# Modulation vectors and x loaded behind the second projection's weights, and queries in tiles of their own, in a two-layer trunk

## The chip, the cores and the metric

The kernel runs on one core of a Trainium2 chip as a single program. The metric is the time of one execution on the device in microseconds, the median of several runs. The kernel before takes 1648.96 us (three runs, 1647.87 to 1651.08).

The core has five engines, each with an instruction stream that is worked off in order: PE (TensorE, matrix products), DVE (VectorE), ACT (ScalarE), POOL (GpSimd) and SP (SyncE, which here only issues transfers). An instruction that waits holds up all that stand behind it on its engine. Work tiles lie in SBUF, products arrive in PSUM, and 16 DMA engines move data between SBUF and the chip's memory (HBM).

## The reference

Two layers over 512 latent tokens and 256 context tokens, width 1024. Layer 0 has a pooling and gated-recurrence mixer, layer 1 attention with grouped keys, normalised queries and keys and rotary positions. Behind each stands a SwiGLU network of hidden width 2816. Norms stand on both sides of each part, and their scale, shift and gate are a modulation worked out from c. Cut to what matters here:

```python
m = silu(c) @ ada_w[l] + ada_b[l]                 # 6 vectors of 1024; for the context from c_ctx
f = swiglu(rmsnorm(x) * (1 + sc2) + sh2, w_in, w_out)
x = x + g2 * rmsnorm(f)                           # end of layer 0
h = rmsnorm(x) * (1 + sc1) + sh1                  # start of layer 1
q, k, v = split(h @ att_w_in)                     # 8 heads of queries, 2 of keys and values, 128 wide
q, k = grid_rope(rmsnorm(q)), grid_rope(rmsnorm(k))
```

## The kernel before

All activations lie with features on partitions and tokens in columns: columns 0 to 256 are the context, 256 to 768 the latent tokens. Each matrix product is three products of rounded halves: with w = whi + wlo and x = hh + hl, `mm3` (L185 to L187) adds whi·hh, whi·hl and wlo·hh in PSUM. Weights are loaded by SyncE as they are into one of four buffers `raw` (`load`, L113) and split there: ScalarE rounds them to `whi` (L641), VectorE subtracts and writes `wlo` (L642), after which the buffer is free. The split halves (a slot) lie in two tiles `w`, every third slot in an extra tile `w3`.

The stretch at issue begins where the hidden columns of layer 0's network are done. 22 blocks of hidden columns were written by SyncE from `gs` to memory (`gd`, L751) and come back as `g`, `hh`, `hl`, loaded by GpSimd (L786, L806). The second projection (`ffn0`) takes them in four chunks of 7, 8, 3 and 4 blocks. In a chunk it goes over eight output blocks n, two to a slot of weights in chunks 0 and 1 (`fo`), and in each over 256 and 512 columns (`outs`). Chunk 0's sums are copied out of PSUM by ScalarE (`y`, L732), those of the later chunks are added by VectorE (`y`, L734). Four PSUM buffers serve this. The context is in chunk 3 the last of three groups of 256 columns.

Beside chunks 0 and 1 VectorE works out 24 of the 48 columns of layer 1's modulation: SyncE loads a block of rows (`adat`, 512 KB) into a `raw` buffer, and VectorE multiplies it with the activated vectors `cb` and sums (L366), twice for the first 16 columns, once for the last 8. The first of two products writes what nobody reads to a second `raw` buffer (`junk`). `load_cb` loads the vectors for both streams to all partitions (L373), and ScalarE activates them (L374). The columns are a generator that `tick` advances by a credit for each piece of matrix work; it sets the program's order, from which a scheduler makes each engine's order.

In chunk 3 each group of columns, when done, goes through the norm of the network's output with the addition to `x` (`x` comes back from memory by a load in `Byg.add`, L80; two buffers for three groups), and then the norm of layer 1's input, which makes `hh` and `hl` (L256, L257). For a norm ScalarE squares (`sq`), VectorE adds (`ss`, L233), PE sums over partitions (L204), GpSimd takes the root (`rr`, L210), PE spreads it (L219), and VectorE scales (`u`). The additions to `x` stand on GpSimd (L298). Then `att_proj` makes queries: for each head and group of 256 columns 24 products, a square `sq` and a scaled copy of PSUM (L910, L912) into a tile that takes over the name `y`. Later the sums of the squares are taken by PE, and the head is rotated: SyncE copies it by parts (`sw`, L880), VectorE multiplies and adds, ScalarE rounds it to `qh`. Four heads of the first latent group come ahead of the second group's.

Of the kernel before, what the change touches and what calls it, by code (L numbers as in the profile page):

```python
# [8 lines left out]
F32 = mybir.dt.float32  # L9
F32R = mybir.dt.float32r  # L10
# [41 lines left out]
class Cols:  # L52


    def __init__(self, c, l):
        self.c, self.l = c, l
# [2 lines left out]
        return self.c[k][:, a:b] if b <= CTX else self.l[k][:, a - CTX:b - CTX]  # L59


class Full:


# [7 lines left out]
class Byg:  # L72


    def __init__(self, pool, tag, bufs):
        self.pool, self.tag, self.bufs, self.t, self.pool_nc = pool, tag, bufs, {}, None

    def add(self, a, src):
        t = self.t[a // 256] = self.pool.tile([128, KD, 256], F32, tag=self.tag, name=self.tag, bufs=self.bufs)
        self.pool_nc.sync.dma_start(out=t, in_=src[:, :, a:a + 256])  # L80
        return t

    def __call__(self, k, a, b):
# [9 lines left out]
class Trunk:  # L93
# [648 lines left out]
    def ffn0(self, y, h, closed, done, top):  # L742

        nc = self.nc
        gd = [self.dp.tile([128, 2, NT], F32, name=f"gd{j}") for j in range(KH)]

        def put(j):
            def f(a, b, src):
                t = self.tmp.tile([128, 2, 384], F32R, tag="gs", name="gs", bufs=2)
                self.split(t[:, 0, :b - a], t[:, 1, :b - a], src)  # L750
                nc.sync.dma_start(out=gd[j][:, :, a:b], in_=t[:, :, :b - a].bitcast(F32))  # L751
            return f

        w3 = self.pool("w3")
        self.w3 = w3.__enter__()
        tmp = self.pool("ftmp")
        self.tmp = tmp.__enter__()
        w = {}
        for i, (a, b) in [(i, g) for i in range(3) for g in G3[:2]] + [(i, G3[2]) for i in range(3)]:
            if a == G3[2][0] and i == 0:  # L760
                self.finish()
                closed()
                tp = self.pool("tx", side="right")
                t = self.wino_x(y, tp.__enter__())
                self.load_cb(self.tmp.tile([128, 1024], F32, name="cb0"), 1024)
            self.finish_for(a, b)
            if i not in w:
                w[i] = self.wslot(self.a["w_fi"][0, i], 2048)
            self.hidden(w[i], h, a, b, put(i))

        def ada1(m0, m1, cost):
            for m in range(m0, m1):
                self.ada_cols(m)
                yield cost

        self.along("ada", ada1(24, 48, 9.0))
        for j in range(3, KH - 1):
            self.wino_hidden(self.wino_w(self.a["w_fi"][0, j]), h, t, put(j))
        self.finish()
        tp.__exit__(None, None, None)  # L780
        self.left = []
        self.np = top.enter_context(self.pool("nrm1", side="right"))
        with self.pool("g2", side="right") as gp:
            def gload(j, k):
                t = gp.tile([128, 2, NT], F32R, tag=f"g{k}", name=f"g{k}")
                nc.gpsimd.dma_start(out=t, in_=gd[j].bitcast(F32R))  # L786
                return t

            def two(ts):
                return [lambda k, a, b, p=p: ts[k][:, p, a:b] for p in range(2)]  # L790

            g = [two([gload(j, j) for j in range(7)])]
            wl = self.wslot(self.a["w_fi"][0, KH - 1], 2048)
            for a, b in SG:
                self.hidden(wl, h, a, b, put(KH - 1))
            tmp.__exit__(None, None, None)
            with self.pool("x2", side="right") as xp:
                x = Byg(xp, "x", 2)
                x.pool_nc = nc
                cb = xp.tile([128, 2048], F32, name="cb1")  # L800
                self.load_cb(cb, 2048)
                self.along("ada", ada1(0, 24, 5.5))
                gb = self.htiles()
                for k in range(KD):
                    for p in range(2):
                        nc.gpsimd.dma_start(out=gb[p](k, 0, NT), in_=gd[7 + k][:, p, :].bitcast(F32R))  # L806
                g.append(gb)
                for ci in range(3):
                    if ci == 2:
                        ts = [gload(15 + k, k) for k in range(7)]  # L810
                        g += [two(ts[:3]), two(ts[3:])]
                    for n in range(KD):
                        if n % PER[FCH[0][ci]] == 0:
                            wo = self.fo(0, ci, n)
                        for a, b in GS:
                            self.outs(0, ci, g[ci], y, n, wo, a, b)
                            self.tick((b - a) * FCH[0][ci] / 800)
                self.finish()
                wo = [self.fo(0, 3, n) for n in (0, 4)]
                h1 = self.htiles()  # L820
                for a, b in GL + GS[:1]:
                    for n in range(KD):
                        self.outs(0, 3, g[3], y, n, wo[n // 4], a, b)
                        self.tick(4 * 0.32)
                    self.along((a, 0), done(x, h1, a, b))
                self.finish()
        self.w3 = None
        w3.__exit__(None, None, None)
        return h1
# [52 lines left out]
        (nc.gpsimd if WE & 4 else nc.vector).tensor_tensor(out=sw, in0=sw, in1=self.sin[:, s], op=ALU.mult)  # L882
        nc.vector.tensor_tensor(out=t, in0=t, in1=sw, op=ALU.add)

    def att_proj(self, h, yp):

        nc, ap = self.nc, self.ap
        self.cos = ap.tile([128, LAT], F32, name="cos")
        self.sin = ap.tile([128, LAT], F32, name="sin")
        nc.sync.dma_start(out=self.cos, in_=self.a["cos"])  # L890
        nc.sync.dma_start(out=self.sin, in_=self.a["sin"])
        self.kh = [ap.tile([128, NT], F32R, name=f"kh{i}") for i in range(ATT_KV)]
        self.kl = [ap.tile([128, NT], F32R, name=f"kl{i}") for i in range(ATT_KV)]
        self.vh = ap.tile([128, NCH, 256], F32R, name="vh")
        self.vl = ap.tile([128, NCH, 256], F32R, name="vl")
        self.rs = ap.tile([128, 2, ATT_H, 4], F32, name="rs")
        self.q = Full(yp, KD, F32, "y")

        def queries(w, hd, a, b):
            pt = self.ps()  # L900
# [155 lines left out]
    def run(self):  # L1056
        tc, nc, a = self.tc, self.nc, self.a
        with self.pool("const") as cp, self.pool("small", 2) as self.sm, self.pool("raw", 4) as self.rawp, \
# [12 lines left out]
            self.kvp.__exit__(None, None, None)  # L1071
            with self.psum(mm=("mm", 4), aux=("aux", 4)):
                self.layer1(mx)
            self.yctx.__exit__(None, None, None)

    def psum(self, **m):
        @contextlib.contextmanager
# [11 lines left out]
    def layer0(self):  # L1089
# [36 lines left out]
        with contextlib.ExitStack() as top:  # L1126
            npool = self.pool("nrm1", side="right")
            self.np = npool.__enter__()
            xpool = self.pool("x", side="right")
            x = Byg(xpool.__enter__(), "x", 3)  # L1130
            x.pool_nc = nc
            y = Full(yp, KD, F32, "y")
            for s, _ in G3:
                x.add(s, a["x"])
# [19 lines left out]
                npool.__exit__(None, None, None)  # L1154

            self.h1 = self.ffn0(y, h, closed, done, top)
            self.kvp = self.pool("kv")
            self.ap = self.kvp.__enter__()
            self.att_proj(self.h1, yp)
            assert not self.ada_left  # L1160

    def layer1(self, mx):
        nc, a = self.nc, self.a
        self.sb = SB2
        with self.pool("nrm2", side="right") as self.np, self.pool("x1", side="right") as xp:
            x = cols(None, xp, KD, F32, "x")
            y = Full(self.yp, KD, F32, "y")
            for k in range(KD):
                nc.sync.dma_start(out=x.l[k], in_=self.xs[:, k, :])
            h = self.htiles()  # L1170
# [162 lines left out]
```

## Time and profile before

| | |
|---|---|
| median of three runs | 1648.96 us (1647.87 to 1651.08) |
| profiled execution | 1650.64 us, its span 1648.6 us |
| PE busy | 1545.3 us, 94% of the span, 10656 matmuls |
| VectorE, ScalarE, GpSimd busy | 1004.0 (61%), 647.0 (39%), 122.6 us (7%) |
| mean granted clock of PE | 0.974 of full speed |
| read and written in memory | 178.28 and 24.64 MB |

PE is near its full time, so the profile is read for the places where PE waits, and for what PE waits for: a line "PE mm L185 <- ACT whi" says that products of line 185 stood until ScalarE's `whi` was there. The granted clock is a share of full speed; 0.50 is 1.2 GHz, 1.00 is 2.4 GHz. Line numbers are those of the kernel before. The mean of a group of rows mixes its forms where it says so.

### The profile page before, as it was taken

Reading aid. Unit: us, or ns where it says so; the run is one execution under the profiler, and the core shown is the slowest. Engines: PE = TensorE matmul, PEld = TensorE weight load, DVE = VectorE, ACT = ScalarE, POOL = GpSimd, SP = SyncE. Lnnn points to the kernel's source line nnn. Section 1 sums busy time; section 2 is a strip of 40 time slices with the busy share of each in tenths; the row PEclk is TensorE's granted clock in tenths of the full one; section 3 lists DMA queues with packets and bytes.
Section 4 is the critical chain, followed back from the end, with each engine's and each line's share of the span. In section 5 each row is a group of like instructions: output and inputs, shape, how many; then the busy total and the mean of one; then the engine's idle time right before and its main releaser. Section 6 shows DMA issues by size and latency. Waiting matters only on the chain.

```text
span 1648.6 us, 26592 instructions
## 1 busy us (share of the span) xinstructions
PE 1545.3 (94%) x10656; PEld 1385.3 (84%) x10656; DVE 1004.0 (61%) x1923; ACT 647.0 (39%) x1228; POOL 122.6 (7%) x163
## 2 busy tenths in 40 slices
PE   5999998999999999999599994999999999999997
PEld 2877776789899999999488894989999888888886
DVE  5366575644789898873465467678947523343345
ACT  3334343254555444442121133457845332222222
POOL 0000000001200000002000013220004000000002
PEclk9999999999999999999799996999999899999998
DMA  9142242341515555438878213230022223322311
GB/s 364 51 154 78 78 129 78 122 154 64 153 66 200 183 191 187 160 129 277 282 252 285 77 40 103 82 111 27 2 103 78 86 93 103 102 92 88 101 52 51
DMA packets 78154, 207.25 MB, mean 126 GB/s; under 512 B 7760, under 2 KB 35920, under 8 KB 77904
## 3 DMA queue, kind: packets, MB, share of 16 engines
q1 hardware_dynamic: 73568, 188.07, 35.1%
q0 software_dynamic: 4320, 17.30, 3.0%
q8 instruction: 83, 1.36, 0.3%
q14 instruction: 39, 0.32, 0.1%
q10 hardware_dynamic: 144, 0.20, 0.0%
HBM read 178.28 MB, written 24.64 MB: 123 GB/s over the span
## 4 chain that ended last, share of the span: by engine, by line
PE 62%; DVE 6%; POOL 2%; ACT 2%; issue 1%; DMA 1%; SPq 0%; POOLq 0%; DVEq 0%; ACTq 0%
PE mm L185 20%; PE mm L186 19%; PE mm L187 19%; DVE ss L233 1%; DMA raw<-adat 1%; PE pp L1022 1%; POOL x L298 1%; PE aux L204 1%; PE aux L219 1%; PE st L185 1%; PE st L187 1%; PE st L186 1%; DVE u L294 0%; DVE wlo L642 0%; POOL rr L210 0%
## 5 line engine op out<-in xcount | busy, mean ns | idle before, releaser
L185 PE MATMUL mm<-hh,whi 128*128 128x256 f32 (+2 forms) x1292 | 431.1, 335 | 9.9 <-ACT y L912 8.7
L187 PE MATMUL mm<-hh,wlo 128*128 128x256 f32 (+2 forms) x1292 | 427.1, 331 | 5.0 <-DVE wlo L642 3.3
L186 PE MATMUL mm<-hl,whi 128*128 128x256 f32 (+2 forms) x1292 | 426.9, 331 | 0.0
L185 PEld LDWEIGHTS mm<-hh,whi 128*128 128x128 f32 x1292 | 247.5, 192 | 39.4 <-ACT y L912 9.0
L187 PEld LDWEIGHTS mm<-hh,wlo 128*128 128x128 f32 x1292 | 247.7, 192 | 23.0 <-DVE wlo L642 3.7
L186 PEld LDWEIGHTS mm<-hl,whi 128*128 128x128 f32 x1292 | 247.8, 192 | 16.5 <-DVE hl L642 0.2
L641 ACT ACTIVATE whi<-raw 128x1024 fp32r<-128x1024 f32 (+2 forms) x145 | 134.1, 945 | 227.9 <-PE mm L186 118.9
L642 DVE TENSOR_TENSOR wlo<-raw,whi 128x1024 fp32r<-128x1024 f32 (+2 forms) x145 | 156.6, 1096 | 70.8 <-ACT whi L641 69.3
L210 POOL TENSOR_TENSOR rr<-rv,mhalf 128x2 f32<-128x2 f32 (+1 forms) x53 | 46.4, 879 | 1122.9 <-DVE rv L207 1105.0
L678 DVE TENSOR_TENSOR sa<-sa,mm 128x256 f32<-128x256 f32 (+2 forms) x38 | 20.7, 546 | 165.3 <-PE mm L187 165.2
L734 DVE TENSOR_TENSOR y<-y,mm 128x256 f32<-128x256 f32 (+1 forms) x104 | 55.9, 542 | 80.3 <-PE mm L187 79.3
L185 PE MATMUL mm<-hh,w3hi 128*128 128x256 f32 (+2 forms) x284 | 94.1, 332 | 2.8 <-ACT w3hi L641 1.4
L187 PE MATMUL mm<-hh,w3lo 128*128 128x256 f32 (+2 forms) x284 | 93.4, 330 | 1.4 <-DVE w3lo L642 1.4
L186 PE MATMUL mm<-hl,w3hi 128*128 128x256 f32 (+2 forms) x284 | 93.7, 331 | 0.0
L641 ACT ACTIVATE w3hi<-raw 128x1024 fp32r<-128x1024 f32 (+2 forms) x51 | 43.2, 875 | 96.3 <-PE mm L186 78.7
L233 DVE TENSOR_TENSOR ss<-ss,sq 128x256 f32<-128x256 f32 x126 | 58.7, 475 | 34.2 <-ACT sq L232 28.9
L185 PE MATMUL mm<-g,whi 128*128 128x256 f32 (+1 forms) x176 | 55.7, 317 | 19.3 <-ACT whi L641 19.3
L366 DVE SCALAR_TENSOR_TENSOR raw<-raw,cb 128x1024 f32<-128x1024 f32 x48 | 58.4, 1220 | 5.5 <-DMA raw<-adat 4.9
L642 DVE TENSOR_TENSOR w3lo<-raw,w3hi 128x1024 fp32r<-128x1024 f32 (+2 forms) x51 | 50.1, 1001 | 16.6 <-ACT w3hi L641 16.6
L185 PEld LDWEIGHTS mm<-hh,w3hi 128*128 128x128 f32 x284 | 54.6, 193 | 6.5 <-ACT q L705 1.7
L187 PEld LDWEIGHTS mm<-hh,w3lo 128*128 128x128 f32 x284 | 54.6, 193 | 4.7 <-DVE w3lo L642 1.6
L186 PEld LDWEIGHTS mm<-hl,w3hi 128*128 128x128 f32 x284 | 54.7, 193 | 3.1
(293 smaller groups left out, 3358.6 us busy)
## 6 DMA issues: line engine op xcount, KB each, us to landing
raw<-w_fi SPq DMA_DIRECT2D x88, 512.0 KB, 4.3
raw<-ada SPq DMA_DIRECT2D x48, 512.0 KB, 5.6
raw<-adat SPq DMA_DIRECT2D x48, 512.0 KB, 4.4
raw<-w_fo SPq DMA_DIRECT2D x40, 512.0 KB, 4.7
gd<-gs SPq DMA_DIRECT2D x38, 384.0 KB, 2.8
g<-gd POOLq DMA_DIRECT2D x14, 768.0 KB, 10.5
raw<-w_ab SPq DMA_DIRECT2D x20, 512.0 KB, 4.9
x<-x SPq DMA_DIRECT2D x9, 1024.0 KB, 8.2
```

The source lines that it names most:

```text
L185: self.nc.tensor.matmul(out=out, lhsT=wh, rhs=xh, start=first and i == 0, stop=False, **kw)
L186: self.nc.tensor.matmul(out=out, lhsT=wh, rhs=xl, start=False, stop=False, **kw)
L187: self.nc.tensor.matmul(out=out, lhsT=wl, rhs=xh, start=False, stop=i == n - 1, **kw)
L204: nc.tensor.matmul(out=pc[:, 2 * t:2 * t + 2], lhsT=ss[:, t * 128:(t + 1) * 128], rhs=self.ones[:, 0:2], start=True, stop=True)
L210: nc.gpsimd.tensor_tensor(out=r[:, :nt], in0=v[:, :nt], in1=self.mhalf[:, :nt], op=ALU.pow)
L219: nc.tensor.matmul(out=pb[:, t * 128:(t + 1) * 128], lhsT=r[:, t:t + 1].to_broadcast([128, 128]), rhs=self.ident, start=True, stop=True)
L233: nc.vector.tensor_tensor(out=ss[:, :n], in0=ss[:, :n], in1=sq[:, :n], op=ALU.add)
L366: nc.vector.scalar_tensor_tensor(out=junk, in0=raw, scalar=1.0, in1=self.cb[:, i * 1024:i * 1024 + 1024], op0=ALU.mult, op1=ALU.mult, accu ...
L641: self.nc.scalar.activation(out=hi, in_=src, func=AF.Copy)
L642: (eng or self.nc.vector).tensor_tensor(out=lo, in0=src, in1=hi.bitcast(F32), op=ALU.subtract)
L678: nc.vector.tensor_tensor(out=s[:, :n], in0=s[:, :n], in1=p[1][:, :n], op=ALU.mult)
L734: nc.vector.tensor_tensor(out=y(n, a, b), in0=y(n, a, b), in1=pt[:, :b - a], op=ALU.add)
```

## The change

It has three parts. First, in `ffn0` the modulation vectors are loaded after the second output block's place in chunk 0 instead of ahead of the chunk, and the generator of columns starts at the fifth block, with a cost of 5.0 for each column instead of 5.5. Second, `x` of the closing norm is loaded by GpSimd instead of SyncE. Third, queries are written to tiles of 128 x 256 of their own, one for each head and group, in the attention's pool; the pool of `y` is closed ahead of it, so that keys and values lie where `y` lay, and layer 1 opens a pool for its own `y`. Tiles of the attention's pool are made in another order. The line numbers of the kernel after are 10 or 11 higher.

```diff
@@ class Groups (new)
+class Groups:
+    def __init__(self, pool, groups):
+        self.t = {a // 256: [pool.tile([128, 256], F32, name=f"q{a // 256}_{k}") for k in range(KD)] for a, _ in groups}
+
+    def __call__(self, k, a, b):
+        return self.t[a // 256][k][:, a % 256:a % 256 + b - a]
@@ class Byg
-    def __init__(self, pool, tag, bufs):
-        self.pool, self.tag, self.bufs, self.t, self.pool_nc = pool, tag, bufs, {}, None
+    def __init__(self, pool, tag, bufs, eng):
+        self.pool, self.tag, self.bufs, self.t, self.eng = pool, tag, bufs, {}, eng
...
-        self.pool_nc.sync.dma_start(out=t, in_=src[:, :, a:a + 256])
+        self.eng.dma_start(out=t, in_=src[:, :, a:a + 256])
@@ ffn0
-                x = Byg(xp, "x", 2)
-                x.pool_nc = nc
+                x = Byg(xp, "x", 2, nc.gpsimd)
                 cb = xp.tile([128, 2048], F32, name="cb1")
-                self.load_cb(cb, 2048)
-                self.along("ada", ada1(0, 24, 5.5))
...
                         if n % PER[FCH[0][ci]] == 0:
                             wo = self.fo(0, ci, n)
+                        if (ci, n) == (0, 1):
+                            self.load_cb(cb, 2048)
+                        if (ci, n) == (0, 4):
+                            self.along("ada", ada1(0, 24, 5.0))
@@ att_proj
-    def att_proj(self, h, yp):
+    def att_proj(self, h):
...
-        self.q = Full(yp, KD, F32, "y")
+        self.q = Groups(ap, GL)
@@ the trunk, before the attention
             self.h1 = self.ffn0(y, h, closed, done, top)
+            self.yctx.__exit__(None, None, None)
             self.kvp = self.pool("kv")
             self.ap = self.kvp.__enter__()
-            self.att_proj(self.h1, yp)
+            self.att_proj(self.h1)
@@ layer1
-        with self.pool("nrm2", side="right") as self.np, self.pool("x1", side="right") as xp:
+        with self.pool("nrm2", side="right") as self.np, self.pool("x1", side="right") as xp, self.pool("y1") as yp:
...
-            y = Full(self.yp, KD, F32, "y")
+            y = Full(yp, KD, F32, "y")
```

SyncE's order from the weights of chunk 0's first slot on, before (`w_fo` weights of the second projection, `gs` hidden columns that are stored, `cb` modulation vectors, `adat` blocks of the modulation, `x_73` the copy of `x` in memory):

```order
L113 DMA raw<-w_fo 128x1024
L113 DMA raw<-w_fo 128x768
L751 DMA gd_4441<-gs 256x1x384 x2
L113 DMA raw<-adat 128x1024
L751 DMA gd_4442<-gs 256x1x384 x2
L751 DMA gd_4443<-gs 256x1x384 x2
L373 DMA cb_8020<-cb 128x2048
L80 DMA x<-x_73 128x8x256 x2
L113 DMA raw<-adat 128x1024 x2
L113 DMA raw<-w_fo 128x1024
L113 DMA raw<-w_fo 128x768
```

and now, where the second and third slot follow the store of `gd_4441`:

```order
L123 DMA raw<-w_fo 128x1024
L123 DMA raw<-w_fo 128x768
L761 DMA gd_4441<-gs 256x1x384 x2
L123 DMA raw<-w_fo 128x1024
L123 DMA raw<-w_fo 128x768
L123 DMA raw<-w_fo 128x1024
L123 DMA raw<-w_fo 128x768
L123 DMA raw<-adat 128x1024
L761 DMA gd_4442<-gs 256x1x384 x2
L761 DMA gd_4443<-gs 256x1x384 x2
L383 DMA cb_8020<-cb 128x2048
L123 DMA raw<-adat 128x1024 x2
```

The weights of the second slot moved from behind `cb`, both `x` and three columns to ahead of the first column, the third slot's with them, and `x` left this engine.

ScalarE's order behind the squares of the context group's norm, before (`sq<-mm` and `y_...<-mm` are the square and the copy of one head of queries, `hh` the context's input of layer 1):

```order
L910 ACTIVATE sq<-mm 128x256
L912 ACTIVATE y_10001<-mm,consts 128x256
L910 ACTIVATE sq<-mm 128x256
L912 ACTIVATE y_10002<-mm,consts 128x256
L910 ACTIVATE sq<-mm 128x256
L912 ACTIVATE y_10003<-mm,consts 128x256
L910 ACTIVATE sq<-mm 128x256
L912 ACTIVATE y_10004<-mm,consts 128x256
L256 ACTIVATE hh_9258<-u,mods_101 128x256
L256 ACTIVATE hh_9259<-u,mods_101 128x256
```

and now:

```order
L921 ACTIVATE sq<-mm 128x256 x4
L266 ACTIVATE hh_9258<-u,mods_101 128x256
L266 ACTIVATE hh_9259<-u,mods_101 128x256
L266 ACTIVATE hh_9260<-u,mods_101 128x256
L266 ACTIVATE hh_9261<-u,mods_101 128x256
L266 ACTIVATE hh_9262<-u,mods_101 128x256
L266 ACTIVATE hh_9263<-u,mods_101 128x256
L266 ACTIVATE hh_9264<-u,mods_101 128x256
L266 ACTIVATE hh_9265<-u,mods_101 128x256
L923 ACTIVATE q_0_10002<-mm,consts 128x256
L923 ACTIVATE q_1_10003<-mm,consts 128x256
```

The four copies moved from beside their squares to behind all eight `hh`; two more copies, of `q_2` and `q_3`, follow directly.

VectorE's order at the first evacuations of chunk 1, before (`y_3498` is output block 0, products with `cb` are those of the columns):

```order
L642 TENSOR_TENSOR wlo<-raw,whi 128x1024 x2
L734 TENSOR_TENSOR y_3498<-y_3498,mm 128x256
L366 SCALAR_TENSOR_TENSOR junk,mods_101<-raw,cb_8020 128x1024
L366 SCALAR_TENSOR_TENSOR raw,mods_101<-raw,cb_8020 128x1024
L366 SCALAR_TENSOR_TENSOR junk,mods_101<-raw,cb_8020 128x1024
L734 TENSOR_TENSOR y_3498<-y_3498,mm 128x512
L366 SCALAR_TENSOR_TENSOR raw,mods_101<-raw,cb_8020 128x1024
L366 SCALAR_TENSOR_TENSOR junk,mods_101<-raw,cb_8020 128x1024
L734 TENSOR_TENSOR y_3499<-y_3499,mm 128x256
```

and now:

```order
L376 SCALAR_TENSOR_TENSOR junk,mods_101<-raw,cb_8020 128x1024
L376 SCALAR_TENSOR_TENSOR raw,mods_101<-raw,cb_8020 128x1024
L744 TENSOR_TENSOR y_3498<-y_3498,mm 128x256
L652 TENSOR_TENSOR w3lo<-raw,w3hi 128x1024 x2
L744 TENSOR_TENSOR y_3498<-y_3498,mm 128x512
L376 SCALAR_TENSOR_TENSOR junk,mods_101<-raw,cb_8020 128x1024
L376 SCALAR_TENSOR_TENSOR raw,mods_101<-raw,cb_8020 128x1024
L744 TENSOR_TENSOR y_3499<-y_3499,mm 128x256
```

Between the first two evacuations a split of weights stands in place of three products, and the columns' products follow in pairs.

## Rows read from the trace of the kernel before

**Rows 1.** Page, costliest groups: count | busy, mean ns | idle before, releaser.

```profile
L185 PE MATMUL mm<-hh,whi 128*128 128x256 f32 (+2 forms) x1292 | 431.1, 335 | 9.9 <-ACT y L912 8.7
...
L185 PE MATMUL mm<-g,whi 128*128 128x256 f32 (+1 forms) x176 | 55.7, 317 | 19.3 <-ACT whi L641 19.3
L366 DVE SCALAR_TENSOR_TENSOR raw<-raw,cb 128x1024 f32<-128x1024 f32 x48 | 58.4, 1220 | 5.5 <-DMA raw<-adat 4.9
```

**Rows 2.** Chain of waits, 755 to 850: start us, length us, what.

```profile
779.04 5.59 SPq L80
784.68 18.56 DMA raw<-adat
...
804.52 3.68 DMA raw<-w_fo
```

**Rows 3.** Windows: length, busy PE PEld DVE ACT POOL, PEclk, DMA share, GB/s.

```profile
790.00:809.30 19.30, 0.08 (x1) 0.00 (x0) 7.31 (x12) 3.17 (x4) 0.00 (x0) 0.59 0.91 305
809.30:813.00 3.70, 3.67 (x15) 3.34 (x16) 3.16 (x3) 0.84 (x1) 0.00 (x0) 0.50 0.66 205
...
848.80:906.00 57.20, 57.20 (x330) 50.53 (x330) 35.21 (x59) 9.52 (x11) 3.77 (x7) 1.00 0.87 304
...
1036.00:1094.00 58.00, 58.00 (x407) 54.15 (x406) 38.25 (x117) 25.54 (x55) 16.26 (x18) 1.00 0.36 102
```

**Rows 4.** Time line of SyncE: start us, length us, instruction.

```profile
748.14 0.33 SPq L113 DMA_DIRECT2D raw<-adat  x1
759.72 17.87 SPq L751 DMA_DIRECT2D gd<-gs  x4
...
813.19 1.60 SPq L113 DMA_DIRECT2D raw<-w_fo  x2
...
825.09 1.56 SPq L113 DMA_DIRECT2D raw<-w_fo  x2
...
991.60 0.52 SPq L80 DMA_DIRECT2D x<-x  x1
```

**Rows 5.** Time line of ScalarE, chunk 0; last column: idle before, releaser.

```profile
789.44 1.91 ACT L374 ACTIVATE cb<-cb 128x2048 f32<-128x2048 f32 x1 [6.15 <-DMA cb<-cb]
...
819.15 0.60 ACT L732 ACTIVATE y<-mm 128x512 f32<-128x512 f32 x1 [1.19 <-PE mm L187]
...
826.57 0.60 ACT L732 ACTIVATE y<-mm 128x512 f32<-128x512 f32 x1 [4.51 <-PE mm L187]
```

**Rows 6.** Time line of VectorE, evacuations of chunk 1.

```profile
878.53 0.68 DVE L734 TENSOR_TENSOR y<-y,mm 128x512 f32<-128x512 f32 x1
...
906.29 0.69 DVE L734 TENSOR_TENSOR y<-y,mm 128x512 f32<-128x512 f32 x1 [4.58 <-PE mm L187]
...
914.63 0.69 DVE L734 TENSOR_TENSOR y<-y,mm 128x512 f32<-128x512 f32 x1 [5.05 <-PE mm L187]
```

**Rows 7.** Time line of PE, fifth query and what stands around it.

```profile
1026.02 0.58 PE L185 MATMUL mm<-hh,whi 128*128 128x256 f32 x1 [8.69 <-ACT y L912]
...
1031.06 0.56 PE L185 MATMUL mm<-hh,whi 128*128 128x256 f32 x1
```

**Rows 8.** Time line of ScalarE in the queries.

```profile
1011.60 0.91 ACT L256 ACTIVATE hh<-u,mods 128x256 fp32r<-128x256 f32 x2 [1.05 <-DVE u L249]
...
1030.44 0.38 ACT L910 ACTIVATE sq<-mm 128x256 f32<-128x256 f32 x1 [3.21 <-PE aux L204]
```

**Rows 9.** Time line of VectorE in the queries.

```profile
996.68 1.74 DVE L642 TENSOR_TENSOR wlo<-raw,whi 128x1024 fp32r<-128x1024 f32 x1
...
1006.36 1.27 DVE L249 SCALAR_TENSOR_TENSOR u<-x,scol,aux 128x256 f32<-128x256 f32 x3 [0.91 <-PE aux L219]
...
1029.80 1.26 DVE L249 SCALAR_TENSOR_TENSOR u<-x,scol,aux 128x256 f32<-128x256 f32 x3 [2.23 <-PE aux L219]
```

**Rows 10.** Time line of GpSimd, a load's issue and the second group's additions.

```profile
785.63 0.54 POOL L806 DMA_DIRECT2D hl<-gd  x1 [0.47 <-DMA hl<-gd]
...
992.10 6.92 POOL L298 TENSOR_TENSOR x<-x,u 128x256 f32<-128x256 f32 x8 [1.55 <-issue]
```

More of the change, by code (lines that the diff above doesn't have):

```diff
@@ L883, in rope @@
         nc.vector.tensor_tensor(out=t, in0=t, in1=sw, op=ALU.add)
-    def att_proj(self, h, yp):
+    def att_proj(self, h):
         nc, ap = self.nc, self.ap
+        self.kh = [ap.tile([128, NT], F32R, name=f"kh{i}") for i in range(ATT_KV)]
+        self.kl = [ap.tile([128, NT], F32R, name=f"kl{i}") for i in range(ATT_KV)]
+        self.vh = ap.tile([128, NCH, 256], F32R, name="vh")
+        self.vl = ap.tile([128, NCH, 256], F32R, name="vl")
         self.cos = ap.tile([128, LAT], F32, name="cos")
@@ L891, in att_proj @@
         nc.sync.dma_start(out=self.sin, in_=self.a["sin"])
[L892 to L895, printed above, removed]
         self.rs = ap.tile([128, 2, ATT_H, 4], F32, name="rs")
-        self.q = Full(yp, KD, F32, "y")
+        self.q = Groups(ap, GL)
         def queries(w, hd, a, b):
@@ L1073, in run @@
                 self.layer1(mx)
-            self.yctx.__exit__(None, None, None)
     def psum(self, **m):
@@ L1129, in layer0 @@
             xpool = self.pool("x", side="right")
-            x = Byg(xpool.__enter__(), "x", 3)
-            x.pool_nc = nc
+            x = Byg(xpool.__enter__(), "x", 3, nc.sync)
             y = Full(yp, KD, F32, "y")
```

## The prediction

> **What bounds the kernel now.** The two lines of PE on the page that waited longest come first [rows 1]: TensorE is busy 94% of the span, so a gain has to be a wait of PE that goes, and a loss one that comes. PE's first product of chunk 0 with the weights `whi` waited 19.3 us for ScalarE's split, once. In the queries it waited 8.7 us for ScalarE's copies `y`, once. The change touches both places.
>
> The chain that ended last says what stood behind the first wait [rows 2]. SyncE is held 5.59 us at the issue of `x`; the load of one modulation column behind it takes 18.56 us; only when VectorE has used that column is a `raw` buffer free for the second slot's weights, which land after 3.68 us, at 808.2, and are split from then on. The windows then show PE empty, 0.08 us busy of 19.30, and its granted clock at 0.50, the 1.2 GHz level, in the next stretch [rows 3]. SyncE's own time line shows room: its last stores of hidden columns stand from 759.72 to 777.6, and a column was loaded as early as 748.14 [rows 4].
>
> The second place is read from the time lines of PE, ScalarE, VectorE and GpSimd [rows 7 to 10]. There the end is set by a serial line (norm of the context group, its modulation, the queries' evacuations), not by PE.
>
> The sum is made against the profiled execution's own 1650.64 us (span 1648.6, 2.0 around it); the median of the runs is 1648.96, 1.7 lower, and the forecast is carried over to it by that difference.
>
> **Weights before modulation.** SyncE's order puts the four loads of the second and third slot between two stores of hidden columns, ahead of the modulation vectors. In time that is behind the store that stood shortly before 748.14. The splits stand on ScalarE and VectorE among the last hidden column's work, the third slot's behind the last product with the slot before it, hence at about 778 at the latest (an estimate from 759.72 + 17.87 [rows 4]). PE wants the second slot at 790.0, the third two steps later. So the 19.3 us go. The low clock goes with them: the step that began at 809.3 ended at 819.15, 9.8 us, where the next took 826.57 - 819.15 = 7.42 [rows 5]: 2.4 us. Together **-21.7 us**. What is late next is the fourth slot. It has to wait for the first columns, which wait for cb: cb was converted at 789.44 + 1.91 = 791.3 [rows 5], and it is issued a few us later now, with no `x` behind it on SyncE. Three columns of two products of 1.22 us [rows 1] end at 798.7, the load takes 3.7, the split some 3 us: about 806 (estimate), wanted at 790.0 + 4 x 7.42 = 819.7. Some 13 us of cover. The 1 to 2 us by which the hidden columns' last stores move back are hidden: their values are first read in chunk 2.
>
> **Modulation beside chunk 1.** The chain of columns starts where it did (at cb), but PE reaches chunk 1 21.7 us sooner. In VectorE's order the evacuations `y` of chunk 1 stand between the columns' products. Before, PE lost nothing there (57.20 busy of 57.20 [rows 3]), although evacuations were late [rows 6]: steps end every 914.63 - 906.29 = 8.34 us, so the one that ran at 878.53 was ready at 906.29 - 4 x 8.34 = 872.9, 5.6 us late. Four PSUM buffers are two steps of two groups, so a step of 8.34 and the small group's share of the next, some 11 us, is what PE can bear. The columns gain ground as well, since no round waits for `x`; rounds of three columns and one slot took 813.19 - 804.5 = 8.7 and 825.09 - 813.19 = 11.9 us on SyncE [rows 2, 4], under a slot's 14.8 (two steps of 7.42) or 16.7 (of 8.34). Bounds 0 (they keep pace) and 6 us (they keep their old times to half of the 21.7, so that lateness goes from 5.6 to 16.5); I take **+1**, near the old row, where nothing was lost.
>
> **Queries in homes of their own.** The values copied are the same. But ScalarE's order differs: before, a square and its copy `y` alternate and all four pairs stand ahead of the last `hh`; now the four squares stand first, then the eight `hh` of the context group, then the four copies `q`. The fifth query needs one of four PSUM buffers, free only after the first copy. Before, that copy ended at 1026.0 and PE began the fifth query at 1026.02, after 8.69 us [rows 7]. It is no gain that this wait changes its name: three products on, PE stood at the norm again and really went on at 1031.06. Now the eight `hh` decide. Their `u` start at 1029.80 [rows 9], the fourth square delays the first `hh` to about 1030.8 [rows 8]; undisturbed, eight `u` and `hh` took from 1006.36 to 1011.60 + 0.91 = 1012.5, 6.15 us [rows 8, 9]. So 1036.0 to 1036.4, then 0.47 for the copy: the fifth query starts near 1037.0, with three products more to do, about 0.6: 1037.0 - 1031.06 + 0.6 = 6.5, less some 0.5 that ScalarE and VectorE save by having nothing else between. **+6**. Behind it PE was full to 1094 (58.00 of 58.00 [rows 3]), so the delay is passed on. Bounds: +4 (the `hh` run closer, as in the undisturbed run with their first at once, and less is lost at the low clock) and +9 (ScalarE now also waits at `qh`, which stands ahead of the keys' weights in its order, for VectorE's rotation of the first head and so for the transfers of `sw`; VectorE's split of those weights stands behind it. That is 1 to 2 us short of being seen by PE, by the time of two queries between).
>
> **x by GpSimd.** Two loads stand behind the 16 of `hh` and `hl`, which ended at 786 [rows 10], and are first read some 170 us later: nothing on the path. The third stands ahead of the second group's additions. It waits for the buffer that SyncE too waited for (it issued this load at 991.60 [rows 4]), so only its own time counts. No row has GpSimd issuing 1024 rows of 1 KB; 128 rows of 3 KB took 0.54 us [rows 10]. Bounds 0.54 and 8 x 0.54 = 4.3 us, against 0.5 that is free before the additions at 992.10 [rows 10]. On the same line VectorE's two splits (1.74 and about 1.2 us) moved from between the sums `ss` to ahead of them [rows 9], which gives back up to 3. So -3 to +4; I take **0**, nearest to the 0.54 row with half of the 3 lost elsewhere.
>
> The Trainium skill, page "DMA: Bandwidth & Descriptors", section "Issuing engines are not separate DMA queues", speaks against this part: loads from any engine run on the same 16 DMA engines, and another issuer saves only the time of issue. By that rule this move alone would be worth the 5.59 us of [rows 2] at most, and here nothing once the weights are ahead of `x`; the sum does not use it.
>
> Sum: -21.7 + 1 + 6 + 0 = -14.7 us; 1650.64 - 14.7 = 1635.9 for a profiled execution, less 1.7: **1634.3 us**.
>
> **The rivals.**
> *The queries cost nothing.* If copies are not held, or the line from 992 to 1031 shortens by the 3 us, the time is 1648.96 - 21.7 - 3 = 1624 to 1648.96 - 21.7 + 1 = 1628, taken as 1627. For it: PE's 8.7 us wait is on the page. Against: in-order ScalarE. Chance 0.14.
> *Another 6 us are lost*, in chunk 1's evacuations, at GpSimd's third load or at the keys' split: the upper bounds above, one at a time: 1640. For it: evacuations 5.6 us late already. Against: no PE wait there before. Chance 0.22.
> *The wait is moved on by two slots* (the change does not do what it says): columns behind cb take 18.56 us each as in [rows 2], because `x`, `hh` and `hl` still move at that time. Two such loads in line after cb give 791.3 + 18.56 + 18.56 + 3 = 831.4 at the fourth slot against 819.7: 12 us, and 2.4 of clock: 1634.3 + 14.4 = 1649. Against: the columns are in flight while cb lands, and `x` is issued later. Chance 0.05.
> *Slower.* SyncE's alternation of three columns and one slot becomes the bound up to chunk 1's end. Four rounds have 14.8 + 3 x 16.7 = 64.9 us; with a round of P the loss is 4P - 64.9, so it decides from 64.9 + 14.7 = 79.6, P = 19.9 us. A round with one load of 18.56 and six products (7.3) in series is 25.9: 38.7 us lost, 1673; with P = 22 it is 1657. Against: the rounds of 8.7 and 11.9. Chance 0.07.
>
> **How the numbers follow.** The forecast has 0.52; its own range is 1630 to 1638. Of the rest, 0.14 lies below and 0.34 above. The range for 8 in 10 takes in the first two rivals but the outer part of each: 1625 to 1643. About 0.2%, 3.3 us, is what a measurement of this kernel can tell from no change. Faster: 0.52 + 0.14 + 0.22 = 0.88. Within: 0.05 from the moved wait. Slower: 0.07.
>
> **What would show it.** In the profile after: no wait of PE for `whi` in chunk 0, the step evacuations 7.42 us apart from the first on and chunk 0's end some 21.7 us sooner; windows of chunk 1 with PE full; in the queries a PE wait of 10 us or so that now names the copy `q`, with the eight `hh` between the squares and the copies; `x` on GpSimd's queue with its duration. Wrong it would be if PE waits at the fourth slot or in chunk 1, if copies run ahead of the `hh`, or if GpSimd's third load takes over 4 us and the second group's additions start late.

## The result, and the profile after

The kernel after takes 1632.55 us (1630.79 to 1633.65, four runs) against 1648.41 us of the kernel before in the same comparison (1644.3 to 1651.08): a ratio of 0.9905 (0.9882 to 0.9928). Faster, as forecast; the forecast of 1634.3 is 1.8 us above it, and the time lies in the likeliest case's own range.

The sum behind it is less good than that. Both kernels issue the same 10656 matmuls, nearly in the same order, so the k-th matmul of one trace can be set against the k-th of the other, counted from the first, which began at 13.5 and 14.0. Where the difference changes, time was lost or won:

| matmul, counted in order | what it is | began at, before | after | difference, from the first matmul on |
|---|---|---|---|---|
| 5850 | chunk 0, ahead of the old wait | 784.4 | 779.1 | -5.8 |
| 5896 | chunk 0, behind the old wait and its low clock | 814.2 | 787.0 | -27.6 |
| 6258 | chunk 1, behind its wait | 877.9 | 855.9 | -22.5 |
| 7072 | norm of the context group | 1014.0 | 992.3 | -22.2 |
| 7096 | sums of squares of the first four heads | 1030.4 | 1014.1 | -16.8 |
| 10656 | last | | | -17.4 |

So the terms came out as -21.8 (forecast -21.7) in chunk 0, +5.2 (+1) in chunk 1, +0.3 (0) on the line of the norms and +5.4 (+6) in the queries, -11.0 together (-14.7; the parts are rounded). The first 5.8 us are not the change's: the profiled execution of before was slow in code that both share. In the traces of all the kernels below, too, that code is faster than in the trace of before, by 1.4 to 7.6 us.

The two lines of PE that stood in [rows 1], on the page of after. The wait for `whi` in chunk 0 is gone, the one for the copy `y` too; 3.2 us for a `y` of VectorE (L744) have come:

```profile
L195 PE MATMUL mm<-hh,whi 128*128 128x256 f32 (+2 forms) x1292 | 430.5, 335 | 4.4 <-DVE y L744 3.2
...
L195 PE MATMUL mm<-g,whi 128*128 128x256 f32 (+1 forms) x176 | 54.5, 310 | 0.0
```

The waits of PE from 760 to 1045, engine and line, what it waited for, us in total, times, longest. The first three belong to norms and queries and make 30.6 us, where the trace of before has 23.8 between 975 and 1045 (8.7, 6.9, 5.1 and 3.1); the last is chunk 1's:

```profile
PE aux L214 <- DVE ss L243: 19.6, 3, 9.0
PE aux L229 <- POOL rr L220: 6.4, 5, 1.8
PE aux L214 <- ACT hh L266: 4.6, 1, 4.6
PE mm L195 <- DVE y L744: 3.2, 1, 3.2
```

SyncE's time line, to be held against [rows 4]: the four loads of the second and third slot begin at 742.85, the first column at 755.63, cb at 779.26, the fourth slot at 792.65:

```profile
742.85 10.28 SPq L123 DMA_DIRECT2D raw<-w_fo  x4
755.63 0.33 SPq L123 DMA_DIRECT2D raw<-adat  x1
...
779.26 0.33 SPq L383 DMA_DIRECT2D cb<-cb  x1
...
792.65 1.56 SPq L123 DMA_DIRECT2D raw<-w_fo  x2
```

ScalarE in chunk 0, against [rows 5]: the third step ends at 792.24, two steps of 7.42 us behind the first at 777.40, and cb is converted at 786.99:

```profile
777.40 0.60 ACT L742 ACTIVATE y<-mm 128x512 f32<-128x512 f32 x1 [4.52 <-PE mm L197]
...
786.99 1.92 ACT L384 ACTIVATE cb<-cb 128x2048 f32<-128x2048 f32 x1 [6.68 <-DMA cb<-cb]
...
792.24 0.60 ACT L742 ACTIVATE y<-mm 128x512 f32<-128x512 f32 x1 [2.58 <-PE mm L197]
```

The windows with the columns of [rows 3] show where PE is empty now: not in chunk 0, but from 845 to 860, in chunk 1 (3.86 of 5.00 and 7.91 of 10.00, the latter at a granted clock of 0.83):

```profile
784.60:795.00 10.40, 10.40 (x66) 9.35 (x65) 4.84 (x8) 3.27 (x4) 0.00 (x0) 1.00 1.08 393
...
845.00:850.00 5.00, 3.86 (x29) 3.50 (x27) 1.23 (x1) 1.94 (x2) 0.00 (x0) 1.00 0.92 328
850.00:860.00 10.00, 7.91 (x31) 6.46 (x32) 9.72 (x17) 0.37 (x2) 0.00 (x0) 0.83 0.54 183
```

VectorE there, against [rows 6]. The second evacuation, of 512 columns, stands behind both splits of the third slot, and they wait for ScalarE:

```profile
842.41 0.41 DVE L744 TENSOR_TENSOR y<-y,mm 128x256 f32<-128x256 f32 x1
847.13 1.23 DVE L652 TENSOR_TENSOR w3lo<-raw,w3hi 128x1024 fp32r<-128x1024 f32 x1 [4.30 <-ACT w3hi L651]
850.21 1.23 DVE L652 TENSOR_TENSOR w3lo<-raw,w3hi 128x1024 fp32r<-128x1024 f32 x1 [1.86 <-ACT w3hi L651]
851.35 0.68 DVE L744 TENSOR_TENSOR y<-y,mm 128x512 f32<-128x512 f32 x1
```

The chain of waits says for what ScalarE waited: a column's load of 8.07 us, then a weight load of 10.45:

```profile
828.03 8.07 DMA raw<-adat
...
838.65 10.45 DMA raw<-w_fo
849.12 1.06 ACT w3hi L651
```

At that time GpSimd had issued the second set of seven loads `g`, from 825.43 on. Its other lines here are the first and the third load of `x`, to be held against [rows 10]:

```profile
783.61 0.92 POOL L90 DMA_DIRECT2D x<-x  x1 [1.95 <-DMA hl<-gd]
...
825.43 1.22 POOL L796 DMA_DIRECT2D g<-gd  x2 [26.86 <-PE mm L197]
...
970.38 0.95 POOL L90 DMA_DIRECT2D x<-x  x1 [1.68 <-ACT hh L266]
```

In the queries ScalarE runs as its order said, against [rows 8]: the fourth square at 1008.71, eight `hh`, and four copies `q` from 1014.41 on:

```profile
1008.71 0.38 ACT L921 ACTIVATE sq<-mm 128x256 f32<-128x256 f32 x1 [3.78 <-PE aux L214]
...
1013.60 0.91 ACT L266 ACTIVATE hh<-u,mods 128x256 fp32r<-128x256 f32 x2 [1.05 <-DVE u L259]
1014.41 1.54 ACT L923 ACTIVATE q<-mm,consts 128x256 f32<-128x256 f32 x4
```

and PE, against [rows 7], takes the sums of the first two heads' squares at 1007.76, waits, takes those of the third and fourth head, and goes on with the fifth query at 1015.80:

```profile
1007.76 1.71 PE L214 MATMUL aux<-ones,sq 128*128 128x2 f32 x8
1014.10 1.83 PE L214 MATMUL aux<-ones,sq 128*128 128x2 f32 x8 [4.63 <-ACT hh L266]
1015.80 0.56 PE L195 MATMUL mm<-hh,whi 128*128 128x256 f32 x1
```

The view names `hh` as what ended the 4.63 us. But the weight load (PEld) of these sums began at 1014.07, and the `hh` named was done only at 1014.11; the last of VectorE's eight `u` was done just before, at 1013.09 + 0.86 = 1013.95. By the kernel's code the sums of the third head take over the PSUM buffer `aux` that the `u` read, the oldest of three:

```profile
1014.07 1.78 PEld L214 LDWEIGHTS aux<-ones,sq 128*128 128x128 f32 x8 [4.69 <-issue]
```

```profile
1013.09 0.86 DVE L259 SCALAR_TENSOR_TENSOR u<-x,scol,aux 128x256 f32<-128x256 f32 x2
```

### The profile page after: what moved, and what is told of

Same layout as the page of the kernel before. It is cut to its first block, busy times and chain, and to the rows that moved or that the text cites. A ratio compares the mean times of both kernels' runs of the same rounds, so it can differ in the third digit from the quotient of the medians.

```text
span 1631.9 us, 26584 instructions
## 1 busy us (share of the span) xinstructions
PE 1538.8 (94%) x10656; PEld 1379.3 (85%) x10656; DVE 1004.2 (62%) x1923; ACT 645.5 (40%) x1228; POOL 123.3 (8%) x166
## 4 chain that ended last, share of the span: by engine, by line
PE 57%; DVE 8%; DMA 4%; ACT 2%; POOL 2%; issue 1%; POOLq 0%; DVEq 0%; ACTq 0%; SPq 0%
PE mm L195 18%; PE mm L196 18%; PE mm L197 18%; DVE ss L243 2%; DMA raw<-adat 1%; DMA gd<-gs 1%; DMA raw<-w_fo 1%; PE pp L1033 1%; POOL x L308 1%; PE aux L214 1%; PE aux L229 1%; POOL rr L220 1%; DVE junk L376 1%; PE st L195 0%; PE st L197 0%
## 5 line engine op out<-in xcount | busy, mean ns | idle before, releaser
L744 DVE TENSOR_TENSOR y<-y,mm 128x256 f32<-128x256 f32 (+1 forms) x104 | 55.9, 542 | 69.2 <-PE mm L197 68.2
L376 DVE SCALAR_TENSOR_TENSOR raw<-raw,cb 128x1024 f32<-128x1024 f32 x48 | 58.6, 1222 | 12.5 <-DMA raw<-adat 11.9
```

The costliest lines, as they stand in the source:

```text
L376: nc.vector.scalar_tensor_tensor(out=junk, in0=raw, scalar=1.0, in1=self.cb[:, i * 1024:i * 1024 + 1024], op0=ALU.mult, op1=ALU.mult, accu ...
L744: nc.vector.tensor_tensor(out=y(n, a, b), in0=y(n, a, b), in1=pt[:, :b - a], op=ALU.add)
```

## The experiments

Ratios are against the kernel before in the same comparison (median 1646.3 to 1647.5 us there).

**Without homes for the queries.** The kernel after with the third part undone:

```diff
-        self.q = Groups(ap, GL)
+        self.q = Full(yp, KD, F32, "y")     # and the pool of y open to the end, tiles in the old order
```

> The kernel after with its third part undone: queries in the tiles of y again, the pool of y open to the end, the attention's tiles in the old order; weights, modulation and x stay as in the kernel after. By the theory the copies q behind the eight hh cost what the traces show between the fifth query and the ones around it, 5.3 us: about 1627 us where the kernel after takes 1632.5, PE going on with the fifth query some 5 us sooner after the last norm, the chunks 0 and 1 as in the kernel after. By the rival (the delay comes from elsewhere on that line, GpSimd's third load or the moved splits, and ScalarE's order does not matter) it stays at 1632 to 1633.

Measured: 1626.52 us (1625.09 to 1629.67), ratio 0.9887 (0.9870 to 0.9904). Against the kernel after PE gains 4.8 us between the last norm's spread and the fifth query, as expected, and no more than 1 us in any other place from 760 to 1070. At the attention's start, from 1077 to 1083, it falls back by 5.2 us and wins 4.2 of them again by 1280; at the end 3.9 us are left of a gain that had come to 4.5. The intervals of the two ratios overlap (0.9870 to 0.9904 here, 0.9882 to 0.9928 for the change), so it is the trace that carries this. The old wait is back and the sum is better:

```profile
PE mm L195 <- ACT y L923: 8.6, 1, 8.6
...
PE mm L195 <- DVE y L744: 2.5, 1, 2.5
```

**Homes alone.** The kernel before with the third part only:

```diff
-        self.q = Full(yp, KD, F32, "y")
+        self.q = Groups(ap, GL)             # and the pool of y closed ahead, as in the change
```

> The kernel before with the third part alone: queries in homes of their own, keys and values where y lay; the modulation ahead of chunk 0 and x on SyncE as before. By the theory it is slower than before by 5 us, about 1653.5 us, with PE's wait before the fifth query near 13 us instead of 8.7 in sum and PE at 0.08 of 19.3 busy in chunk 0 as before. By the rival (homes help or are neutral, since what is undone elsewhere hides them) 1646 to 1649.

Measured: 1649.03 us (1647.33 to 1655.98), ratio 1.0028 (1.0016 to 1.0041), so 2.6 to 6.8 us slower; in the trace 4.8 us are lost at the same place, and the 19.6 us in chunk 0 stay. The wait before the fifth query was expected as one of 13 us; the trace shows none of that name. The waits for the norms' sums and for `hh` now make 16.0 + 4.6 = 20.6 us, where those for the norm's sum and the copy had made 6.9 + 8.7 = 15.6:

```profile
PE mm L195 <- ACT whi L651: 19.6, 1, 19.6
PE aux L214 <- DVE ss L243: 16.0, 2, 9.1
...
PE aux L214 <- ACT hh L266: 4.6, 1, 4.6
```

**Four homes.** The first experiment with homes in the attention's pool for four tiles only:

```diff
-        self.q = Full(yp, KD, F32, "y")
+        yq = Full(yp, KD, F32, "y")
+        own = [ap.tile([128, 256], F32, name=f"q{k}") for k in range(4)]
+        self.q = lambda k, a, b: own[k][:, a - 256:b - 256] if k < 4 and b <= 512 else yq(k, a, b)
```

> The kernel of the first experiment (no homes) with homes in the attention's pool for four tiles only, the first four heads of the first group; all other queries in the tiles of y, whose pool stays open. ScalarE's order then again has the four squares, the eight hh, and only then the four copies. By the theory (a copy whose home lies in a pool that opens after the last norm is placed behind that norm, and this alone costs) PE loses some 5 us at the fifth query against the first experiment: about 1631.5 us where that had 1626.5. By the rival (closing the pool of y, or the other twelve homes and the waits for them, cost the time) it stays at 1626 to 1628.

Measured: 1632.86 us (1628.62 to 1633.92), ratio 0.9905 (0.9887 to 0.9922), and 4.8 us lost at the same place against the first experiment. The intervals of the ratios overlap here too (0.9870 to 0.9904 for the first experiment), so again the trace carries it. Neither closing the pool of `y` nor the other twelve homes is needed for the loss; four homes in the attention's pool, which opens behind the last norm, are enough. Whether it is the pool or the new tile as such, no run here tells apart.

```profile
PE aux L214 <- ACT hh L266: 4.6, 1, 4.6
```

**x on SyncE.** Only the first part of the change:

```diff
-                x = Byg(xp, "x", 2, nc.gpsimd)
+                x = Byg(xp, "x", 2, nc.sync)      # on the first experiment
```

> The kernel after with parts two and three undone, so only the first part on the kernel before: the weights ahead of the modulation, x loaded by SyncE, where it stands between cb and the columns. By the theory that the second part is worth nothing on the path, within 2 us of the run with parts one and two: about 1627 us. By the rival the 5 to 6 us that SyncE is held at x come back as a wait of PE in chunk 0 or 1: 1632 us or more.

Measured: 1628.5 us (1626.31 to 1629.09), ratio 0.9897 (0.9881 to 0.9914), beside 0.9887 (0.9870 to 0.9904): no difference that can be told. PE's waits in chunks 0 and 1 are no longer than with `x` on GpSimd:

```profile
PE mm L195 <- DVE y L744: 2.2, 2, 1.2
```

**x alone on GpSimd.** The kernel before with the second part only (the same line, the other way).

> The kernel before with the second part alone: x loaded by GpSimd, behind its 16 loads of hh and hl; modulation ahead of the weights as before. Before, SyncE was held 5.59 us at x, and the column's load behind it took 18.56 us. By one theory (the issue alone cost) the wait of 19.3 us in chunk 0 shrinks by about 5.6 us: 1641 us where before has 1646.5. By the other (the column landed late because x moved ahead of it on the same DMA engines) the column lands in 10 us or less and the wait shrinks by 12 us or more: 1634 us or less. If neither, 1646.

Measured: 1640.88 us (1638.74 to 1643.92), ratio 0.9966 (0.9955 to 0.9977). PE's wait falls from 19.3 to 13.0 us, by 6.3 us, which is as long as the issue of `x` had held SyncE (5.59 and 0.68). But neither theory came out whole. Counted from the issue of cb, the column's load behind it was issued 6.4 us sooner, and it also landed in 13.0 us instead of 18.56: `x`, which GpSimd issues from 789.38 on, now moves behind it. So the column no longer ends the chain; cb, its conversion, the first column's products and the weights do, and the weights, issued 9.8 us sooner, took 7.24 us instead of 3.68:

```profile
raw<-adat SPq DMA_DIRECT2D x1, 512.0 KB, 13.0
```

```profile
776.25 11.24 DMA cb<-cb
...
793.23 7.24 DMA raw<-w_fo
800.48 1.06 ACT whi L651
```

```profile
PE mm L195 <- ACT whi L651: 13.0, 1, 13.0
```

So the gain is the size of the issue, but it was not won by the issue alone: how much of it the issue made, and how much the bytes that move later, is not told apart here. Once the weights stand ahead of `x`, both are hidden.

**The second set of g on SyncE.** The kernel after with

```diff
-                    ts = [gload(15 + k, k) for k in range(7)]
+                    ts = [gload(15 + k, k, nc.sync) for k in range(7)]
```

> The kernel after, with the second set of seven loads g of 768 KB issued by SyncE instead of GpSimd, where they stand behind the third weight slot of chunk 1 and between modulation columns; VectorE's order then has only one of the two splits of that slot ahead of the second evacuation. In the kernel after PE loses 5.2 us in chunk 1: the second evacuation runs at 851.35, 13.5 us late, behind a split of weights whose load, issued at 837.42, took 8 to 11 us beside those seven loads. By the theory (that load beside the seven, and the split ahead of the evacuation) the 5 us go: about 1627.5 us, PE full in chunk 1. By the rival (VectorE's products for the columns alone make the evacuations late) it stays at 1632 to 1633, and slower if the columns wait for SyncE.

Measured: 1628.9 us (1628.28 to 1631.19), ratio 0.9901 (0.9886 to 0.9917); in the trace PE is full in chunk 1 and wins back the 5.1 us that the kernel after lost there. The medians differ by 3.7 us, the intervals of the two ratios overlap, so it is the trace that carries this. The second evacuation runs at 838.99, behind one split instead of two:

```profile
837.84 1.23 DVE L652 TENSOR_TENSOR w3lo<-raw,w3hi 128x1024 fp32r<-128x1024 f32 x1 [2.21 <-ACT w3hi L651]
838.99 0.68 DVE L744 TENSOR_TENSOR y<-y,mm 128x512 f32<-128x512 f32 x1
```

This moved the loads and VectorE's order at once. The next two kernels keep the order of the kernel after and tell them apart.

**Half of g.**

```diff
-                    ts = [gload(15 + k, k) for k in range(7)]
+                    ts = [gload(15 + k, k, 1) for k in range(7)]     # t[:, :1] <- gd[j][:, :1]
```

> The kernel after with half the bytes in the second set of the seven loads g: only the upper halves are loaded, 384 KB each instead of 768, and chunks 2 and 3 use them in place of the lower halves too, so part of the products is left out. Every engine's order around the wait in chunk 1 is that of the kernel after. By the theory (the third slot's weights and the columns land late because those loads move at the same time) the two weight loads land in 4 to 6 us instead of 8 to 11, the second evacuation of chunk 1 runs 3 us or more sooner, and PE's wait of 3.2 us for it is gone or under 1 us. By the rival (VectorE's products alone) the wait stays near 3 us.

Measured: 1627.91 us in the one execution. The two loads of the third slot's weights were issued at 830.19 instead of 837.42, since the columns ahead of them had landed sooner, and landed in 7.3 us in the median instead of 9.5 (columns: count, KB each, median us to landing; after first, then this one); 4 to 6 had been expected. The evacuation runs at 841.30 instead of 851.35 behind both splits, and PE waits nowhere in chunk 1. This trace came to chunk 1 2.3 us sooner; counted from the same product ahead of it, the 6100th matmul in order, the evacuation comes 20.2 us on instead of 28.0:

```profile
raw<-w_fo SPq DMA_DIRECT2D x2, 512.0 KB, 9.5
```

```profile
raw<-w_fo SPq DMA_DIRECT2D x2, 512.0 KB, 7.3
```

```profile
830.19 1.55 SPq L123 DMA_DIRECT2D raw<-w_fo  x2
```

```profile
841.30 0.68 DVE L744 TENSOR_TENSOR y<-y,mm 128x512 f32<-128x512 f32 x1
```

**Short products.** VectorE's first product of each of 16 columns over 32 elements instead of 1024:

```diff
+            w = 32 if m < 16 and not i else 1024
-            nc.vector.scalar_tensor_tensor(out=junk, in0=raw, ...
+            nc.vector.scalar_tensor_tensor(out=junk[:, :w], in0=raw[:, :w], ...
```

> The kernel after with the first of the two products of each of the first 16 modulation columns cut to 32 of 1024 elements (the context's modulation is left out): VectorE does about half the work for the columns, in the same order, with the same loads and buffers. By the theory of late loads PE's wait in chunk 1 stays, 2 to 3.5 us, since what stands ahead of the second evacuation is a split that waits for its load. By the rival (VectorE's products) the wait is gone.

Measured: 1633.29 us in the one execution. The evacuation runs at 851.92, no sooner than in the kernel after, with VectorE idle ahead of the splits; PE waits 1.7 us for it, a little less than expected. This trace came to chunk 1 2.1 us later than that of after. Counted from the 6100th matmul the evacuation comes 26.4 us on. Kernels with the same chunk 1 as the kernel after have 28.0 (after), 27.2 (without homes) and 25.4 (four homes), with waits of PE of 3.2, 2.5 and 0.9 us: one execution differs from the next by that much, and the short products lie among them, where half of g with its 20.2 does not.

```profile
850.78 1.23 DVE L653 TENSOR_TENSOR w3lo<-raw,w3hi 128x1024 fp32r<-128x1024 f32 x1 [1.87 <-ACT w3hi L652]
851.92 0.68 DVE L745 TENSOR_TENSOR y<-y,mm 128x512 f32<-128x512 f32 x1
```

```profile
PE mm L195 <- DVE y L745: 1.7, 1, 1.7
```

So the late loads decide, and the time of VectorE's products does not.

**Both undone.** The first and the fourth edit together.

> Both losses undone together: the kernel after without homes for the queries (as the first experiment) and with the second set of loads g on SyncE (as the fourth). If the two are independent, as the theory has it, their gains add: 1632.5 - 5 - 4 = about 1623 us against the kernel before at 1646 to 1648, with PE full in chunk 1 and the fifth query's wait as in the kernel before. If the one hides the other (rival), it stays at 1626 to 1628.

Measured: 1623.58 us (1623.19 to 1626.55), ratio 0.9860 (0.9844 to 0.9877), against 0.9905 (0.9882 to 0.9928) of the change. It is the fastest kernel run here, and its interval lies below that of the change. The gains add, as expected, or nearly: from chunk 0 on (the 5850th matmul) to the last, the trace of the change wins 11.6 us against that of before, without homes 17.5, with g on SyncE 16.3, with both 21.2; that is 5.9 and 4.7 alone, and 9.5 together.

**Everything on SyncE.** That kernel with `x` on SyncE too.

> The kernel of the seventh experiment (no homes, second set of g on SyncE) with x on SyncE too, so that of the whole change only the first part is left, beside g. If x on GpSimd is worth nothing on the path, as the third experiment says, 1622 to 1625 us. The rival: SyncE, which now issues everything, is held and the columns fall behind in chunk 1: 1627 us or more, with a wait of PE there.

Measured: 1626.19 us (1625.92 to 1629.05), ratio 0.9874 (0.9858 to 0.9891). Its median is 1.2 us above the range expected, its interval overlaps that of the kernel before it, and PE waits nowhere in chunk 1, so the rival's wait did not come. Nor do the traces show a gain by `x` on GpSimd: from chunk 0 on this one wins 21.4 us against that of before, and the one with `x` on GpSimd 21.2. Whether it is worth a microsecond in the median stays open.

## Why the prediction was right, and where it was not

**Weights before modulation: right.** Forecast -21.7, measured -21.8; the wait and the low clock behind it went as worked out. The fourth slot, feared to be late, was issued at 792.65, was split by 802 (estimate 806) and cost nothing. The moved wait and the slower case, which had SyncE's rounds as the bound, did not come: weights were issued at 792.65, 809.11, 821.92, 837.42 and 856.00, so rounds took 12.8 to 18.6 us, longer than the 8.7 and 11.9 that I argued with, but short of 19.9.

**Modulation beside chunk 1: the step that was mis-sized.** I took +1 within bounds of 0 and 6; it was +5.2. "I take +1, near the old row, where nothing was lost" priced lateness by the old trace's, and the reason given, "the columns gain ground as well", looked at the wrong thing. VectorE's order had shown a part of it: a split of weights stands between the first two evacuations, where there were products before. A split waits for its weights to land, and so can a product for its column: with `x` on SyncE products still stand between those two evacuations, and they waited 4.2 us for a column. What I left out is what moves at that time. Chunk 1's start is just when chunk 0's buffers come free and GpSimd sends seven loads of 768 KB, so the third slot's weights took 9.5 us. PE stopped at 852.09 - 3.23 = 848.86, three groups (11.1 us) behind the one whose evacuation ran at 851.35: 13.6 us late, where four PSUM buffers are good for the 11 us that I had worked out. Half the bytes took the wait away, half the products did not. The size differs between executions: with the same chunk 1, 4.4 us were lost without homes and 1.8 with four homes, so +5.2 is the dear end of it, but no trace with these loads on GpSimd and at full size, and the weights ahead, has less than 1.8. PE waiting in chunk 1 was one of the prediction's own signs of being wrong, and its rival of another 6 us came true there in part.

**Queries: right in size, and in mechanism but for the last link.** Forecast +6, measured +5.4 in the change, and 4.8 of it, the wait itself, in each of the three comparisons that undo or make it. The last norm's spread began at 1028.48 and 1006.75, 21.7 us apart; the working's 1037.0 becomes 1015.3 by that, and the fifth query began at 1015.80. But it was not the first copy `q` that let it go, as I had worked out: that was done at 1014.86. PE's own order now has the sums of the third and fourth head ahead of the fifth query, and these stood until VectorE's last `u` had left their PSUM buffer. So `u`, `hh` and copies do decide the time to within 0.9 us (an estimate, 1015.80 - 1014.9), and the sums the rest. That the size fits so well is luck in part: the working did not know of those sums, which make the query later but are also 1.7 us of work that is then done. The rival of a free evacuation is out.

**x by GpSimd: right.** Forecast 0; on the line from the second group's additions to the context's norm 0.3 us. The third load's issue took 0.95 us, near the lower bound of 0.54 and far from 4.3. The Trainium skill, page "DMA: Bandwidth & Descriptors", section "Issuing engines are not separate DMA queues", says that another issuer saves only the time of issue: the trace of `x` alone agrees in the sum, with 6.3 us saved where SyncE had been held 6.3, but not in its parts, since the column's load also landed 5.6 us faster; and once the weights stood ahead nothing was saved.

**The carried difference.** Of 1650.64 us in the profiled execution I took 1.7 off to reach the median. The trace shows 5.8 us in shared code, and larger samples of the kernel before had medians of 1646.3 to 1647.5. So the terms, 3.7 us too favourable, and a base taken some 2 us too high made up for each other in part; the closeness of 1634.3 to 1632.55 is partly luck, the more so as one execution's loss in chunk 1 differs from the next one's by some 3 us.

## What to carry to other kernels

A wait that goes brings the work behind it forward, into whatever transfers run at that time; look up which burst will then stand beside which load, and in an in-order engine's list, whether what stands ahead of an evacuation is work on hand or work that waits for a load. A copy into a new home can cost by its place in the order: here four homes in a pool opened behind the last norm put four copies behind eight other instructions, and sums ahead of the next query, for 5 us. Before a profiled execution's sum is carried to a median, set the shared stretches of two executions against each other.

## What the runs showed of the hardware that was not expected

`x`, a load of 1 MB with rows of 1 KB in the kernel's view, moves in fewer packets when GpSimd issues it. The page's queues (packets, MB, share of 16 engines), before and then after:

```profile
q1 hardware_dynamic: 73568, 188.07, 35.1%
q0 software_dynamic: 4320, 17.30, 3.0%
```

```profile
q1 hardware_dynamic: 70448, 184.92, 34.3%
q0 software_dynamic: 5136, 20.45, 3.5%
```

With three such loads moved, SyncE's queue lost 3120 packets (1040 each) and GpSimd's gained 816 (272 each), for the same bytes. The issue took 0.90 to 0.95 us on GpSimd, against 5.59 and 0.68 for the two on SyncE beside other traffic, and 0.52 for the third there [rows 4]; so GpSimd's issue is not the shorter one at a quiet place. The load's landing took 10.3 us in the median of two against 21.8 before; they ran at different times, so how much of that is the packets' is not shown.
